# A dense gate matrix built by one-hot matmuls in place of adding scatters, in a Trainium2 encoder layer with product-key experts

## The chip, the cores and the metric

One core of one Trainium2 chip. The metric is device time in microseconds (us) for one execution of the program, taken as the median of several runs.

## The reference, cut to what matters

One encoder layer runs on two sequences, "s" (512 tokens) and "p" (256 tokens), model width 1024. Attention comes first; the part that matters here is the expert layer behind it:

```python
s1 = einsum('thc,hkc->thk', q[:, :, 0], sub_keys_1); s2 = ...    # 8 heads, 128 keys each
v1, i1 = top_k(s1, 16); v2, i2 = top_k(s2, 16)
cand = (v1[..., :, None] + v2[..., None, :]).reshape(T, 8, 256)
top, ci = top_k(cand, 16)
idx = e1 * 128 + e2                     # 8 x 16 = 128 experts of 16384, per token
g = softmax(top)                        # over the 16 of a head
a = gelu(einsum('ted,td->te', expert_u[idx], t))
out = einsum('te,ted->td', g * a, expert_v[idx])
```

For every token 128 of the 16384 experts are chosen, each with a gate g. An expert has a row of u and a row of v, 1024 numbers (4 KB) each.

## The kernel before, in words

**Fronts.** `front("p")` and then `front("s")` do norms, projections, attention, gates, output projection and the query projection of the expert layer. Large products are made of three matmuls (`mm3`, lines 141 to 144): every float32 operand is split by `split` (lines 136 to 139) into a rounded part (ScalarE, line 137) and a rest (VectorE or GpSimd, line 138). At the end of a front `top16` (lines 615 to 621) picks the best 16 of 128 keys for each of 16 half-heads and each tile of 128 tokens.

**Two ways through the experts.** The 256 tokens of p are done by gathers: for each of 2 token tiles, 128 steps fetch one u row for each of 128 tokens (an indirect DMA of 128 x 4 KB, line 782) and reduce it with VectorE (line 789), then 128 steps fetch v rows and accumulate them (line 797). That is 512 gathers. The 512 tokens of s are done densely: stage 1 (`stage1`, lines 714 to 725) computes all 16384 activations in 128 blocks of u, 24 matmuls of 128x512 each, and writes them to `ad` in DRAM; stage 2 (`dense`, lines 727 to 770) reads `ad`, multiplies it with the gate matrix `gd` (line 746) and multiplies by the v blocks, again 128 blocks of 24 matmuls, into eight PSUM tiles `held`.

**The gate matrix.** `gd` holds for every token and expert the gate or zero, 33.5 MB in DRAM, one tensor for each of 4 token tiles. `clear` (lines 700 to 710) fills it with zeros by 16 GpSimd DMAs of 2 MB, woven into the front of p. `pick` (lines 632 to 686), called once for each quarter of the half-heads, makes the indices `si` and gates `wt`; its VectorE steps are the sums `cand` (line 642), `top16`, and for each pair of heads `eq` (line 667), `pr` (line 669) and a reduction (line 670). `scatter` (lines 690 to 698) then issues 512 indirect DMAs from GpSimd's queue, each adding 128 gates of 4 bytes to `gd` (line 696). Stage 2 reads `gd` for 4 blocks at a time (`GRP`), by four DMAs of 256 KB on SyncE's queue (line 737).

**What sets the order.** The program is written as generators that are woven into one another by hand-set rates, and a scheduler then fixes the order of each engine's queue from its own model of times; on the chip each queue is in order. `fill(front("s"), gg, ...)` advances the gathers by 2.25 for every unit of front work. Then 8 blocks of stage 1 are issued (`U0`), the four picks of s carry stage 1 along at 0.45 a unit (`UP`), the 128 steps of four scatters each carry 0.64 blocks of stage 1 (`US`) and 0.44 gathers (`GU`), and the rest of stage 1 follows (lines 848 to 864). `fill(dense(...), gg, GV)` advances 2.2 gathers a v block, and `run(gg)` issues what is left of them. Each gather waits, by a dependence added for pace (line 785), for the last activation that was issued on ScalarE before it. Gathers write into 3 buffers before stage 2 and into 8 in it.

## Time and profile before

| | us |
|---|---|
| median of 3 runs | 2974.01 (2971.81 to 2974.4) |
| the profiled execution, its own time | 2969.84 |
| its span, first to last instruction | 2968.1 |
| mean granted TensorE clock over the span | 0.898 of full speed |

The profiled execution lies 4.2 us under the median, and its time is 1.7 us over its span. PE is the matmul engine TensorE, PEld its weight loads, DVE is VectorE, ACT is ScalarE, POOL is GpSimd, SP is SyncE; a name with a q is the queue of that engine. Matmuls are pipelined and their ends are modelled, so the duration of one is longer than the distance between two.

### The profile page before, as it was taken

Reading aid. Unit: us, or ns where it says so; the run is one execution under the profiler, and the core shown is the slowest. Engines: PE = TensorE matmul, PEld = TensorE weight load, DVE = VectorE, ACT = ScalarE, POOL = GpSimd, SP = SyncE. Lnnn points to the kernel's source line nnn. Section 1 sums busy time; section 2 is a strip of 40 time slices with the busy share of each in tenths; the row PEclk is TensorE's granted clock in tenths of the full one; section 3 lists DMA queues with packets and bytes.
Section 4 is the critical chain, followed back from the end, with each engine's and each line's share of the span. In section 5 each row is a group of like instructions: output and inputs, shape, how many; then the busy total and the mean of one; then the engine's idle time right before and its main releaser. Section 6 shows DMA issues by size and latency. Waiting matters only on the chain.

```text
span 2968.1 us, 31969 instructions
## 1 busy us (share of the span) xinstructions
PE 2334.2 (79%) x10890; PEld 1907.7 (64%) x10890; DVE 1792.2 (60%) x3717; ACT 814.0 (27%) x1315; POOL 1633.8 (55%) x1099
## 2 busy tenths in 40 slices
PE   6899869999987999103666667767999999999950
PEld 5777858778876778102555555555788888888840
DVE  5655896676889992001121212223369989989999
ACT  4554335444322332000111111112222222322210
POOL 0000200555554888888888888886045445544456
PEclk8999989999989999656888888888999999999985
DMA  7875523677862557224565555557679999999999
GB/s 253 284 259 174 161 68 105 206 219 269 283 200 61 121 124 154 18 0 68 115 133 114 127 122 124 116 126 220 222 293 404 402 403 403 394 402 395 397 368 359
DMA packets 311683, 643.06 MB, mean 217 GB/s; under 512 B 98144, under 2 KB 120288, under 8 KB 311520
## 3 DMA queue, kind: packets, MB, share of 16 engines
q0 software_dynamic: 155904, 302.32, 35.4%
q1 hardware_dynamic: 137184, 305.15, 29.7%
...
q14 instruction: 78, 0.64, 0.1%
...
## 4 chain that ended last, share of the span: by engine, by line
PE 32%; POOL 26%; DVE 16%; DMA 14%; issue 10%; ACT 2%; SPq 0%; ACTq 0%; POOLq 0%; DVEq 0%
POOL gd L696 23%; PE held L142 5%; PE held L143 5%; PE held L144 5%; DMA vr<-v 4%; DVE x L797 3%; DMA gr<-u,pidx 2%; DMA wraw<-w_in 2%; POOL gr L782 2%; PE pu L144 2%; DVE gr L789 2%; PE pu L142 2%; PE pu L143 2%; DMA gl<-ad 2%; DMA gd<-wt,si 1%
## 5 line engine op out<-in xcount | busy, mean ns | idle before, releaser
L696 POOL DMA_INDIRECT gd<-wt,si x512 | 881.9, 1722 | 157.1 <-issue 151.8
L144 PE MATMUL pu<-tTh,ul 128*128 128x512 f32 x1024 | 437.6, 428 | 386.5 <-DVE ul L138 386.3
L789 DVE SCALAR_TENSOR_TENSOR gr<-gr,tok 128x1024 f32<-128x1024 f32 x256 | 328.8, 1289 | 489.7 <-DMA gr<-u,pidx 489.1
L782 POOL DMA_INDIRECT gr<-u,pidx x256 | 307.8, 1202 | 419.4 <-ACT ph L137 142.4
L144 PEld LDWEIGHTS pu<-tTh,ul 128*128 128x128 f32 x1024 | 210.0, 205 | 459.2 <-DVE ul L138 414.6
L797 DVE SCALAR_TENSOR_TENSOR x<-gr,act,x 128x1024 f32<-128x1024 f32 x256 | 328.1, 1282 | 289.2 <-DMA gr<-v,pidx 286.1
L782 POOL DMA_INDIRECT gr<-v,pidx x256 | 297.1, 1161 | 321.3 <-ACT ph L137 214.8
L142 PE MATMUL pu<-tTh,uh 128*128 128x512 f32 x1024 | 428.2, 418 | 15.1 <-ACT uh L137 15.1
L143 PE MATMUL pu<-tTl,uh 128*128 128x512 f32 x1024 | 425.0, 415 | 0.0
L143 PE MATMUL held<-vl,ph 128*128 128x512 f32 x1024 | 398.4, 389 | 0.0
L144 PE MATMUL held<-vh,pl 128*128 128x512 f32 x1024 | 398.3, 389 | 0.0
L137 ACT CAST uh<-ur 128x1024 fp32r<-128x1024 f32 x128 | 134.4, 1050 | 905.3 <-PE pu L143 889.0
L142 PE MATMUL held<-vh,ph 128*128 128x512 f32 x1024 | 278.4, 390 | 3.4 <-ACT vh L137 2.7
L138 POOL TENSOR_TENSOR wlo<-wraw,whi 128x1024 fp32r<-128x1024 f32 x51 | 129.8, 2547 | 232.6 <-ACT whi L137 216.4
L142 PEld LDWEIGHTS pu<-tTh,uh 128*128 128x128 f32 x1024 | 210.8, 206 | 60.5 <-ACT uh L137 16.8
L143 PEld LDWEIGHTS pu<-tTl,uh 128*128 128x128 f32 x1024 | 209.8, 205 | 47.8
L142 PEld LDWEIGHTS held<-vh,ph 128*128 128x128 f32 x1024 | 192.0, 188 | 44.7 <-ACT vh L137 3.9
L138 DVE TENSOR_TENSOR ul<-ur,uh 128x1024 fp32r<-128x1024 f32 x128 | 154.0, 1219 | 106.6 <-ACT uh L137 106.6
L144 PEld LDWEIGHTS held<-vh,pl 128*128 128x128 f32 x1024 | 192.3, 188 | 39.9
L143 PEld LDWEIGHTS held<-vl,ph 128*128 128x128 f32 x1024 | 192.2, 188 | 39.9
L137 ACT CAST ph<-gl 128x512 fp32r<-128x512 f32 x128 | 79.6, 622 | 472.3 <-DVE gl L746 402.9
L137 ACT CAST whi<-wraw 128x1024 fp32r<-128x1024 f32 x137 | 143.2, 1048 | 183.6 <-DMA wraw<-w_in 51.5
...
## 6 DMA issues: line engine op xcount, KB each, us to landing
ur<-ublk SPq DMA_DIRECT2D x128, 512.0 KB, 4.0
vr<-v SPq DMA_DIRECT2D x128, 512.0 KB, 11.7
wraw<-w_in SPq DMA_DIRECT2D x80, 512.0 KB, 4.5
...
gt<-gd SPq DMA_DIRECT2D x128, 256.0 KB, 9.1
gl<-ad SPq DMA_DIRECT2D x128, 256.0 KB, 11.2
wraw<-w_query SPq DMA_DIRECT2D x32, 512.0 KB, 4.0
wraw<-w_out SPq DMA_DIRECT2D x16, 512.0 KB, 4.2
```

What stands on the lines that cost most here:

```text
L137: i = ac.copy(hi, src)
L138: eng.tensor_tensor(lo, src, hi.bitcast(F32), op=ALU.subtract)
L142: pe.matmul(out, lhsT=lh, rhs=rh, start=first, stop=False)
L143: pe.matmul(out, lhsT=lh, rhs=rl, start=False, stop=False)
L144: pe.matmul(out, lhsT=ll, rhs=rh, start=False, stop=last)
L696: gp.indirect_dma_start(out=gd[t], out_offset=bass.IndirectOffsetOnAxis(ap=si[:, k:k + 1], axis=0), in_=wt[:, k:k + 1], in_offset=None, co ...
L782: st = gp.indirect_dma_start(out=g, out_offset=None, in_=tab, in_offset=bass.IndirectOffsetOnAxis(ap=pidx[t][:, s:s + 1], axis=0))
L789: ve.scalar_tensor_tensor(g, g, 1.0, tok, op0=ALU.mult, op1=ALU.mult, accum_out=act[:, s:s + 1])
L797: ve.scalar_tensor_tensor(xt, g, act[:, s:s + 1], xt, op0=ALU.mult, op1=ALU.add)
```

## The change

The zero fill and the 512 scatters are gone, and so is `islice`. `pick` now takes one token tile with all 8 heads instead of all token tiles with two heads (the result tiles `vv` and `iu` are laid out to match), two of its steps (`ce` and `pr`) go from VectorE to GpSimd, and it ends with the first index, the second index and the gate of each choice, turned by TensorE so that the choices lie on partitions and the tokens on columns (`sl`). A new function `gbuild` makes, for each token, a 128x128 matrix of first index against second index as one float32 matmul of two one-hot matrices over the 128 choices: `o1` (first index, on VectorE, for 8 tokens at a time) and `o2` (second index times the gate), of which in each 8 tokens 5 are made on VectorE by one instruction and 3 on ScalarE by two. ScalarE copies four tokens out of PSUM together, and each 32 tokens are written to `gd` by one DMA of 2 MB on ScalarE's queue. The order is three picks, a build, a pick, three builds (`ORDER`); a build yields 0.6 for every 4 tokens, which carries 0.6 blocks of stage 1 (`UB`) and 0.9 gathers (`GB`), the latter with 3 more buffers. `gd` is laid out as [16 chunks of 32 tokens, 128, 128, 32], and stage 2 reads it for 8 blocks at a time by one DMA of 2 MB. In stage 2 the gathers have 12 buffers instead of 8, and the pools lie elsewhere in SBUF.

```diff
-GRP = 4
-GR2 = 5
+GCH = 32
+GRP = 8
...
+BY = "avvavvav"
+B1, B2, B3 = 3, 8, 6
...
-U0, UP, US, GU = (8, 0.45, 0.16, 0.11)
-GV = 2.2
+ORDER, SLB = ('pppbpbbb', 3)
+U0, UP, UB = (8, 0.45, 1.0)
+GB, GV = (1.5, 2.2)
...
-    pcol = cp.tile([128, 1], F32, name="pcol")
+    iota = cp.tile([128, 128], F32, name="iota")
...
     sgd = dr.tile([2, 2, 4, 128, 512], F32, name="sgd")
-
-    gd = [dr.tile([128 * 128 * 128, 1], F32, name=f"gd{t}") for t in range(4)]
+    gd = dr.tile([S_S // GCH, 128, 128, GCH], F32, name="gd")
...
-    def pick(pool, seq, c, vv, iu):
...
+    def pick(pool, seq, t, vv, iu):
...
         for i, n in enumerate(CAND[:8]):
-            ve.tensor_tensor(ce[:, :, pos:pos + n], fi[:, :, 1, 0:n], i1[:, :, i:i + 1].broadcast_to([128, n2, n]), op=ALU.add)
+            gp.tensor_tensor(ce[:, :, pos:pos + n], fi[:, :, 1, 0:n], i1[:, :, i:i + 1].broadcast_to([128, 8, n]), op=ALU.add)
             pos += n
-        ve.tensor_tensor(ce[:, :, pos:pos + 8], i1[:, :, 8:16], fi[:, :, 1, 0:1].broadcast_to([128, n2, 8]), op=ALU.add)
...
-        for h in range(n2):
+        for h in range(8):
...
+        for h in range(0, 8, 2):
+            eq = pool.tile([128, 2, NCAND, 16], BF16, tag="eq", name="eq", bufs=2 if seq == "s" else 1)
+            pr = pool.tile([128, 2, 16, NCAND], F32, tag="pr", name="pr", bufs=2 if seq == "s" else 1)
             ve.tensor_tensor(eq, posx.unsqueeze(1).broadcast_to([128, 2, NCAND, 16]),
                              tf[:, h:h + 2, :].unsqueeze(2).broadcast_to([128, 2, NCAND, 16]), op=ALU.is_equal)
-            ve.tensor_tensor(pr, eq.rearrange("p h c s -> p h s c"), ce[:, h:h + 2, :].unsqueeze(2).broadcast_to([128, 2, 16, NCAND]), op=ALU.mult)
+            gp.tensor_tensor(pr, eq.rearrange("p h c s -> p h s c"), ce[:, h:h + 2, :].unsqueeze(2).broadcast_to([128, 2, 16, NCAND]), op=ALU.mult)
             ve.tensor_reduce(ex[:, h:h + 2, :], pr, op=ALU.add, axis=AX.X)
...
-        wt = pool.tile([128, n2, 16], F32, tag=f"wt{c}", name="wt", bufs=1)
-        ve.tensor_tensor(wt, tv, tv[:, :, 0:1].broadcast_to([128, n2, 16]), op=ALU.subtract)
-        gates(pool, wt, n2)
-        si = pool.tile([128, n2 * 16], I32, tag=f"si{c}", name="si", bufs=1)
-        ve.tensor_scalar(si, ex.rearrange("p h s -> p (h s)"), 128.0, pcol, op0=ALU.mult, op1=ALU.add)
-        slots[c] = (si, wt.rearrange("p h s -> p (h s)"))
...
+        ei = pool.tile([128, 128], I32, tag="ei", name="ei", bufs=1)
+        ve.tensor_copy(ei, ex.rearrange("p h s -> p (h s)"))
+        ii = pool.tile([128, 128], I32, tag="ii", name="ii", bufs=1)
+        for z in range(2):
+            if z == 0:
+                ve.tensor_single_scalar(ii, ei, 7, op=ALU.logical_shift_right)
+            else:
+                ve.tensor_single_scalar(ii, ei, 127, op=ALU.bitwise_and)
+            ve.tensor_copy(e[z].rearrange("p h s -> p (h s)"), ii)
+        p = ps_tr("p_sl")
+        for j, src in enumerate((e[0], e[1], wt)):
+            pe.transpose(p[:, j * 128:(j + 1) * 128], src.rearrange("p h s -> p (h s)"), ident)
+        sl[t] = [slp[0].tile([128, 128], F32, tag=f"sl{j}", name=f"sl{j}", bufs=SLB) for j in range(5)]
+        for j in range(3):
+            ac.copy(sl[t][j], p[:, j * 128:(j + 1) * 128])
+        for j in range(1, 3):
+            ac.mul(sl[t][2 + j], p[:, j * 128:(j + 1) * 128], -1.0)
         yield 2
 
...
-    def scatter(c):
-
-        si, wt = slots[c]
-        for s in range(32):
-            for t in range(4):
-                k = t * 32 + s
-                gp.indirect_dma_start(out=gd[t], out_offset=bass.IndirectOffsetOnAxis(ap=si[:, k:k + 1], axis=0),
-                                      in_=wt[:, k:k + 1], in_offset=None, compute_op=ALU.add)
-            yield 1
...
-    def clear():
-
-        z = gpl.tile([128, D], F32, tag="gr", name="zero", bufs=3)
-        gp.memset(z, 0.0)
-        for t in range(4):
-            v = gd[t].rearrange("(p q k d) o -> q p k (d o)", p=128, q=4, d=D)
-            for q in range(4):
-                st = gp.dma_start(v[q], z.unsqueeze(1).broadcast_to([128, 4, D]))
-                if anchor[0] is not None:
-                    tc.add_manual_dep(st.ins, anchor[0].ins.name, SYNC, reason="pace")
-                yield 0
+    def gbuild(pool, t):
+        for c in range(128 // GCH):
+            gs = pool.tile([128, 128, GCH], F32, tag="gs", name="gs", bufs=2)
+            for q in range(0, GCH, 4):
+                p = (ps_tr, ps_o)[q // 4 % 2]("p_g")
+                t4 = c * GCH + q
+                if q % 8 == 0:
+                    o1 = pool.tile([128, 8, 128], F32, tag="o1", name="o1", bufs=B1)
+                    ve.tensor_tensor(o1, iota.unsqueeze(1).broadcast_to([128, 8, 128]),
+                                     sl[t][0][:, t4:t4 + 8].unsqueeze(2).broadcast_to([128, 8, 128]), op=ALU.is_equal)
+                for j in range(4):
+                    tk = t4 + j
+                    tg = {"a": "o2a", "v": "o2"}[BY[tk % len(BY)]]
+                    o2 = pool.tile([128, 128], F32, tag=tg, name=tg, bufs=B2 if tg == "o2" else B3)
+                    if tg == "o2a":
+                        ac.activation(o2, iota, AF.Abs, bias=sl[t][3][:, tk:tk + 1])
+                        ac.activation(o2, o2, AF.Relu, bias=sl[t][2][:, tk:tk + 1], scale=sl[t][4][:, tk:tk + 1])
+                    else:
+                        ve.tensor_scalar(o2, iota, sl[t][1][:, tk:tk + 1], sl[t][2][:, tk:tk + 1], op0=ALU.is_equal, op1=ALU.mult)
+                    pe.matmul(p[:, j * 128:(j + 1) * 128], lhsT=o1[:, q % 8 + j, :], rhs=o2, start=True, stop=True)
+                ac.copy(gs[:, :, q:q + 4].rearrange("p e t -> p t e"), p.rearrange("p (t e) -> p t e", e=128))
+                yield 0.6
+            nc.scalar.dma_start(gd[t * (128 // GCH) + c], gs)
...
-                for t in range(4):
-                    nc.sync.dma_start(gts[g][:, t], gd[t].rearrange("(p e t) o -> p e (t o)", e=128, t=128)[:, g * GRP:(g + 1) * GRP, :])
+                gts[g] = pv_.tile([128, S_S // GCH, GRP, GCH], F32, tag="gt", name="gt", bufs=2)
+                nc.sync.dma_start(gts[g], gd[:, :, g * GRP:(g + 1) * GRP, :].rearrange("c p e t -> p c e t"))
...
-            gv = ga.rearrange("p (t k) -> p t k", k=128)
+            gv = ga.rearrange("p (c t) -> p c t", t=GCH)
...
-            more = len(gp2) and s % (GR2 + 3) >= 3
-            g = (gp2[0] if more else pool).tile([128, D], F32, tag="gr2" if more else "gr", name="gr", bufs=GR2 if more else 3)
+            more, n = gp2[-1]
+            own = s % (n + 3) < 3
+            g = (pool if own else more).tile([128, D], F32, tag="gr" if own else "gr2", name="gr", bufs=3 if own else n)
...
     gpl = ctx.enter_context(tc.tile_pool(name="ga", bufs=1, side="right", reuse_waits="tile"))
-    zero = clear()
-    fill(front("p"), zero, 0.5)
-    run(zero)
+    run(front("p"))
     def picks_p():
-        for c in range(4):
-            yield from pick(pks["p"][1], "p", c, *tops["p"][c])
+        for t in range(2):
+            yield from pick(pks["p"][1], "p", t, *tops["p"][t])
         pks["p"][0].__exit__(None, None, None)
...
-    due, gdue = [0.0], [0.0]
-    for c in range(4):
-        fill(pick(pks["s"][1], "s", c, *tops["s"][c]), ua, UP, due)
-    for c in range(4):
-        for _ in scatter(c):
-            due[0] += US * 4
-            gdue[0] += GU * 4
-            while due[0] >= 1.0:
-                due[0] -= 1.0
-                next(ua, None)
-            while gdue[0] >= 1.0:
-                gdue[0] -= 1.0
-                next(gg, None)
-    run(ua)
+    with tc.tile_pool(name="gb", bufs=1, reuse_waits="tile") as gpool:
+        slp.append(gpool)
+        gp2.append((gpool, 3))
+        P = [pick(pks["s"][1], "s", t, *tops["s"][t]) for t in range(4)]
+        B = [gbuild(gpool, t) for t in range(4)]
+        due = [0.0]
+        it = {"p": iter(P), "b": iter(B)}
+        for k in ORDER:
+            g = next(it[k])
+            fill(weave(g, gg, GB) if k == "b" else g, ua, UP if k == "p" else UB, due)
+        run(ua)
+        gp2.append((None, 0))
     pks["s"][0].__exit__(None, None, None)
     psx[0].__exit__(None, None, None)
-    gp2.append(ctx.enter_context(tc.tile_pool(name="gr2", bufs=1, side="right", reuse_waits="tile")))
+    ux.__exit__(None, None, None)
+    gp2.append((ctx.enter_context(tc.tile_pool(name="gr2", bufs=1, reuse_waits="tile")), 9))
     psd = ctx.enter_context(tc.tile_pool(name="psd", bufs=1, space=PSUM))
-    pv_ = ctx.enter_context(tc.tile_pool(name="dv", bufs=1, reuse_waits="tile"))
+    pv_ = ctx.enter_context(tc.tile_pool(name="dv", bufs=1, side="right", reuse_waits="tile"))
     fill(dense(pv_, psd), gg, GV)
     run(gg)
```

## Rows read from the trace of the kernel before

**Rows 1.** Windows: length, busy time (x instructions) of PE, PEld, DVE, ACT, POOL, clock, DMA share, GB/s.

```profile
966.00:1196.00 230.00, 218.42 (x943) 176.53 (x943) 162.35 (x452) 72.10 (x94) 199.81 (x100) 0.99 0.60 133
1196.00:1369.00 173.00, 1.69 (x8) 1.07 (x6) 0.00 (x0) 1.54 (x2) 144.65 (x94) 0.52 0.23 2
1369.00:2047.00 678.00, 467.73 (x1706) 364.30 (x1706) 145.87 (x148) 109.77 (x143) 568.55 (x360) 0.85 0.58 123
2047.00:2160.00 113.00, 103.91 (x432) 83.37 (x431) 41.42 (x39) 30.49 (x40) 14.40 (x11) 0.96 0.68 244
2160.00:2862.00 702.00, 697.18 (x3072) 576.13 (x3070) 627.75 (x779) 199.47 (x251) 346.00 (x279) 1.00 1.01 390
2862.00:2968.00 106.00, 0.00 (x0) 0.00 (x0) 99.66 (x79) 0.00 (x0) 70.96 (x69) 0.52 0.94 369
```

**Rows 2.** Waits from 1380 to 2047 us: engine line, whom for, total us, times, longest.

```profile
DVE x L797 <- DMA gr<-v,pidx: 274.5, 26, 15.9
DVE gr L789 <- DMA gr<-u,pidx: 252.5, 23, 15.8
...
PE pu L144 <- DVE ul L138: 195.3, 48, 8.0
```

**Rows 3.** Groups by form: busy us, mean ns of one, idle before and its releasers.

```profile
L696 POOL DMA_INDIRECT gd<-wt,si x512 | 881.9, 1722 | 157.1 <-issue 151.8 <-DMA gd<-wt,si 4.0 <-DVE vv L620 1.3
...
L137 ACT CAST uh<-ur 128x1024 fp32r<-128x1024 f32 x128 | 134.4, 1050 | 905.3 <-PE pu L143 889.0 <-PE pu L144 6.6 <-DVE ti L618 4.4
...
L138 POOL TENSOR_TENSOR wlo<-wraw,whi 128x1024 fp32r<-128x1024 f32 x51 | 129.8, 2547 | 232.6 <-ACT whi L137 216.4 <-DVE iu L621 5.3 <-DVE vv L617 5.3
L138 DVE TENSOR_TENSOR wlo<-wraw,whi 128x1024 fp32r<-128x1024 f32 x86 | 109.5, 1276 | 88.4 <-ACT whi L137 87.9
...
L669 DVE TENSOR_TENSOR pr<-eq,ce 128x1600 f32<-128x1600 bf16 x24 | 79.3, 3303 | 0.0
...
L439 ACT ACTIVATE sm<-sm,nm 128x256 f32<-128x256 f32 x56 | 28.4, 507 | 37.7 <-DVE nm L488 20.5 <-DVE nm L515 11.2 <-DVE es L525 3.3
...
L609 ACT COPY ss<-p_s 128x512 f32<-128x512 f32 x16 | 9.4, 587 | 58.4 <-DVE s L619 47.5 <-PE p_s L607 10.9
```

**Rows 4.** Timeline of PE around four float32 matmuls of 128x128 (start, us, instruction).

```profile
948.13 1.05 PE L607 MATMUL p_s<-kys,qT 128*128 128x128 f32 x8
948.94 0.48 PE L144 MATMUL pq<-tTh,wlo 128*128 128x512 f32 x1
949.25 0.40 PE L142 MATMUL pq<-tTh,whi 128*128 128x512 f32 x1
```

**Rows 5.** Instructions on single tiles: duration ns min/median/max, first and last start.

```profile
L138 DVE TENSOR_TENSOR ul<-ur,uh x128: 1192/1220/1285, 967.6 to 2149.0; 128x1024 fp32r<-128x1024 f32 x128
...
L684 DVE TENSOR_SCALAR si<-ex,pcol x4: 256/268/344, 945.4 to 1110.2; 128x128 int32<-128x128 f32 x4
...
L642 DVE TENSOR_TENSOR cand<-vv x64: 142/173/2405, 318.1 to 1049.8; 128x16 f32<-128x16 f32 x16, 128x8 f32<-128x8 f32 x12, 128x32 f32<-128x32 f32 x8, 128x64 f32<-128x64 f32 x8
```

**Rows 6.** Gathers issued: up to 945, 1370 to 2047 (two), from 2860 (durations ns, starts).

```profile
L782 POOL DMA_INDIRECT gr<-u,pidx x104: 932/940/1987, 500.9 to 859.8; - x104
...
L782 POOL DMA_INDIRECT gr<-v,pidx x26: 997/1000/1003, 1698.2 to 2039.5; - x26
L782 POOL DMA_INDIRECT gr<-u,pidx x23: 1000/1001/1009, 1387.6 to 1688.2; - x23
...
L782 POOL DMA_INDIRECT gr<-v,pidx x70: 936/1016/1861, 2859.5 to 2954.9; - x70
```

**Rows 7.** DMA issues (count, KB, median us to landing): 0 to 220 us, 220 to 500, 500 to 950.

```profile
wraw<-w_in SPq DMA_DIRECT2D x39, 512.0 KB, 6.5
...
wraw<-w_in SPq DMA_DIRECT2D x26, 512.0 KB, 3.7
...
gr<-u,pidx POOLq DMA_INDIRECT x104, 5.6
```

**Rows 8.** Waits of the first 220 us: engine line, whom for, total us, times, longest.

```profile
ACT whi L137 <- DMA wraw<-w_in: 41.3, 16, 4.7
```

More of the change, by code (lines that the diff above doesn't have):

```diff
@@ L1 @@
 from contextlib import ExitStack
-from itertools import islice
 import numpy as np
@@ L581, in front @@
             pp = fs.enter_context(tc.tile_pool(name="wq" + seq, bufs=1, side="right" if seq == "p" else "left", reuse_waits="tile"))
-            vv = [pk.tile([128, nt, 4, 16], F32, tag=f"vv{c}", name="vv") for c in range(4)]
-            iu = [pk.tile([128, nt, 4, 16], U32, tag=f"iu{c}", name="iu") for c in range(4)]
+            vv = [pk.tile([128, 16, 16], F32, tag=f"vv{t}", name="vv") for t in range(nt)]
+            iu = [pk.tile([128, 16, 16], U32, tag=f"iu{t}", name="iu") for t in range(nt)]
             for c in range(4):
@@ L610, in front @@
                     for t in range(nt):
-                        top16(pp, ss[:, t, :], 128, vv[c][:, t, m, :], iu[c][:, t, m, :])
+                        top16(pp, ss[:, t, :], 128, vv[t][:, hh, :], iu[t][:, hh, :])
                     yield 0
@@ L621, in top16, with gates @@
         ve.max_index(out=i[:, 8:16], in_max=v[:, 8:16], in_values=s2[:, :n])
-    def gates(pool, w, n=8):
+    def gates(pool, w):
         ac.activation(w, w, AF.Exp)
-        sm = pool.tile([128, n], F32, tag="gsm", name="gsm", bufs=1)
+        sm = pool.tile([128, 8], F32, tag="gsm", name="gsm", bufs=1)
         ve.tensor_reduce(sm, w, op=ALU.add, axis=AX.X)
         ve.reciprocal(sm, sm)
-        ve.tensor_tensor(w, w, sm.unsqueeze(2).broadcast_to([128, n, 16]), op=ALU.mult)
-    def pick(pool, seq, c, vv, iu):
-        nt = 4 if seq == "s" else 2
-        n2 = 2 * nt
-        fi = pool.tile([128, n2, 2, 16], F32, tag="fi", name="fi", bufs=1)
-        ac.copy(fi.rearrange("p h z k -> p (h z) k"), iu.rearrange("p t m k -> p (t m) k"))
-        v4 = vv.rearrange("p t (h z) k -> p (t h) z k", z=2)
-        cand = pool.tile([128, n2, NCAND], F32, tag="cand", name="cand", bufs=1)
+        ve.tensor_tensor(w, w, sm.unsqueeze(2).broadcast_to([128, 8, 16]), op=ALU.mult)
@@ L640, in pick @@
+    def pick(pool, seq, t, vv, iu):
+        fi = pool.tile([128, 8, 2, 16], F32, tag="fi", name="fi", bufs=1)
+        ac.copy(fi.rearrange("p h z k -> p (h z) k"), iu)
+        v4 = vv.rearrange("p (h z) k -> p h z k", z=2)
+        cand = pool.tile([128, 8, NCAND], F32, tag="cand", name="cand", bufs=1)
         pos = 0
         for i, n in enumerate(CAND[:8]):
-            ve.tensor_tensor(cand[:, :, pos:pos + n], v4[:, :, 1, 0:n], v4[:, :, 0, i:i + 1].broadcast_to([128, n2, n]), op=ALU.add)
+            ve.tensor_tensor(cand[:, :, pos:pos + n], v4[:, :, 1, 0:n], v4[:, :, 0, i:i + 1].broadcast_to([128, 8, n]), op=ALU.add)
@@ L650, in pick @@
+        tv = pool.tile([128, 8, 16], F32, tag="tv", name="tv", bufs=1)
+        ti = pool.tile([128, 8, 16], U32, tag="ti", name="ti", bufs=1)
+        ce = pool.tile([128, 8, NCAND], F32, tag="ce", name="ce", bufs=1)
+        i1 = pool.tile([128, 8, 16], F32, tag="i1", name="i1", bufs=1)
         ac.mul(i1, fi[:, :, 0, :], 128.0)
@@ L672, in pick @@
         if seq == "p":
-            for t in range(nt):
-                k = slice(32 * c, 32 * c + 32)
-                h = slice(2 * t, 2 * t + 2)
-                ve.tensor_tensor(pw[t][:, k].rearrange("p (h s) -> p h s", s=16), tv[:, h, :], tv[:, h, 0:1].broadcast_to([128, 2, 16]), op=ALU.subtract)
-                ve.tensor_copy(pidx[t][:, k], ex[:, h, :].rearrange("p h s -> p (h s)"))
+            ve.tensor_tensor(pw[t].rearrange("p (h s) -> p h s", s=16), tv, tv[:, :, 0:1].broadcast_to([128, 8, 16]), op=ALU.subtract)
@@ new lines, in pick @@
+        ve.tensor_tensor(wt, tv, tv[:, :, 0:1].broadcast_to([128, 8, 16]), op=ALU.subtract)
+        gates(pool, wt)
+        ei = pool.tile([128, 128], I32, tag="ei", name="ei", bufs=1)
+        ve.tensor_copy(ei, ex.rearrange("p h s -> p (h s)"))
+        ii = pool.tile([128, 128], I32, tag="ii", name="ii", bufs=1)
+        for z in range(2):
+            if z == 0:
[3 more added lines that the diff above has]
+            ve.tensor_copy(e[z].rearrange("p h s -> p (h s)"), ii)
@@ L923, in _layout @@
     o["posx"] = np.broadcast_to(np.arange(NCAND).astype(ml_dtypes.bfloat16)[:, None], (128, NCAND, 16))
-    o["pcol"] = np.arange(128, dtype=np.float32)[:, None]
+    o["iota"] = np.broadcast_to(np.arange(128, dtype=np.float32), (128, 128))
     o["maskA_s"], o["maskB_s"], o["maskO_s"] = _masks(_SEQ_S, _PERM_S[:128], 4)
```

33 lines of the change are left out of this document (17 added, 16 removed).

## The prediction

> **What bounds the kernel now.** I read the windows by stage first, then the waits of the longest stage, then the costs of single groups. The windows [rows 1] show that the stretch between the fronts and stage 2, from 966 to 2160 us, takes 1194 us for work that TensorE does elsewhere in little over half of that: stage 2 has the same 3072 matmuls of 128x512 and does them in 702 us, 0.229 us each, at clock 1.00 (2.4 GHz). In the stretch there are three different states. Up to 1196 stage 1 runs beside the picks at 943 matmuls in 230 us, 0.244 us each. From 1196 to 1369 TensorE, VectorE and ScalarE all stand still, and the granted clock of idle TensorE is 0.52, close to the lower of its two levels (1.2 GHz). From 1369 to 2047 TensorE has 1706 matmuls in 678 us, 0.397 us each, at 0.85, while GpSimd is busy for 569 of them.
>
> Who holds whom is in the waits [rows 2]: VectorE waits 274.5 and 252.5 us for gathered rows, and TensorE waits for `ul`, a VectorE product that stands behind those waits in VectorE's queue. The gathers are late because they stand in GpSimd's queue among the scatters, 512 of 1.72 us with 157.1 us of idle time before them, 2.03 us each [rows 3]. So the scatters pace the stretch through the gathers, and TensorE is not the bound. Once the last scatter is out at 2047, the remaining matmuls go at 432 in 113 us, 0.262 us each [rows 1]. Stage 2 is bound by TensorE and by transfers nearly equally (DMA share 1.01), and behind it stands a tail of 106 us in which only gathers run [rows 1].
>
> **The change, part by part.** *The stretch.* The scatters go, 1039 us of GpSimd time. What is late next is TensorE. Its work is 128 blocks of 24 matmuls and 512 new float32 matmuls of 128x128, in 128 groups of four. The trace has four matmuls of this form in one piece (eight records) [rows 4]: from their start to the start of the second matmul behind them are 1.12 us, of which one 128x512 matmul takes 0.23, so a group of four costs 0.89. The bounds are 0.81 (to the start of the first matmul behind) and 1.05 (the piece's own length). At the full rate the work is 702 + 128 x 0.89 = 816 us. I take the rate at which stage 1 ran beside the picks, 0.244 instead of 0.229, because there too VectorE and ScalarE had much other work: 3072 x 0.244 + 114 x 0.244/0.229 = 871 us, and 3 for twelve transposes, 874. Gain: 1194 - 874 = **320 us**.
>
> This holds if no other engine needs more. VectorE: `ul` 128 x 1.22 = 156 us; `o1` is a two-input operation of the same shape, 64 x 1.22 = 78; `o2` is nearest to the 128x128 operation with a scalar, 320 x 0.268 = 86 [rows 5]; gathers, 112 at no more than 106/70 = 1.5 us (the tail over its gathers), 168 [rows 1, 6]; picks and `top16` no more than the 162 us of the first window less the `ul` of its 39 blocks, 115 [rows 1]. That is 603 of 874. ScalarE: 128 casts of 1.05 and as many activations of 128x512, about 0.59 like the copy, 210 us; 192 tokens with two instructions, each at most the 0.507 of the 128x256 activation with its own bias, 195; 128 copies of 0.587, 75 [rows 3]; 480 of 874. The copies write with a stride of 128 bytes, which no row shows: as fast as the copy, or, bounded by the slowest row of that group, 1.05 us each, 60 us more, which still hides. GpSimd: the gathers and 16 products `pr`. A product costs 3.30 us on VectorE, and the same subtraction is 2547 ns on GpSimd against 1276 on VectorE [rows 3], so 6.6 us, 106 us together, hidden behind stage 1 as long as VectorE, which waits for each, has other work queued. Transfers: u 67 MB, `ad` 34, the new `gd` writes 34, gathers 112 x 0.52 = 58; 193 MB in 874 us is 221 GB/s, against 390 in stage 2 [rows 1]. On SyncE's queue 128 reads of `gd` become 16; on ScalarE's queue 16 writes of 2 MB are added, each behind the copy that fills it, so ScalarE waits for nothing there.
>
> *Gathers.* The fronts issued 104 [rows 6]. The picks of p now make 22 steps instead of 24, so two more fit, 106. The scatters carried 128 x 0.44 = 56, the builds carry 28 each, 112. Stage 2 carries 281 in both. So 106 + 112 + 281 = 499 of 512 are out by its end and 13 are left where 70 were. They came out at 95.4 us for 70, 1.36 us each [rows 6], so the tail of 106 us loses 57 x 1.36 = **77 us** and 29 remain.
>
> *Stage 2.* The matmuls are the same. The reads of `gd` come as 2 MB every 8 blocks in pieces of 1 KB, before as four times 256 KB every 4 blocks in pieces of 2 KB; with more gather buffers the transfers may start earlier. TensorE is hardly ever short of data now. I take **5 us more**. The bounds: no change below, and above, if these 33.5 MB took twice as long as at 390 GB/s, 86 us more, since transfers already fill the stage [rows 1].
> The page DMA: Bandwidth & Descriptors of the Trainium skill (Latency and other measured facts) says that copies whose row pitch is a large power of two lose bandwidth, 164 GB/s at 2 MiB against 207 at 512 KiB. In the new layout 16 pieces lie 2 MiB apart for each partition, so by that rule the 86 us would become about 108, an estimate of 22 us more from that page's figures; no run here shows such a pitch yet.
>
> *Front of p.* Its transfers lose 33.5 MB of zeros. The weight tiles landed in 6.5 us there and in 3.7 behind it [rows 7], and ScalarE waited 41.3 us for them [rows 8]. I take 15 us of gain, 41.3 x (1 - 3.7/6.5) = 18 less a little, as some of these waits are hidden; bounds 0 and 41. `pr` of the p picks, 8 products, goes to GpSimd with one buffer: 8 x 3.3 us less on VectorE against 8 x 6.6 that it waits; -26 to +26 us, taken as nothing, since fronts have other work for VectorE.
>
> *Sum.* 2968 - 15 - 320 + 5 - 77 = 2561 us of span; the profiled execution would be 1.7 above it, 2563, and the median of the runs shown lies 4 above the profiled execution: **2567 us**.
>
> **The rivals.** *Build stalls.* Every group of four needs three engines in turn, and all queues are in order. If TensorE were fed only 80% of the time, the stretch would be 816/0.8 = 1020 us, 146 more: 2713. For it: at 0.262 us a matmul the end of the stretch ran at 87% even without scatters. Against it: 0.244 beside saturated picks, and stage 2 at full rate with VectorE busy 628 of 702 us [rows 1].
>
> *The picks wait for GpSimd.* VectorE then pays 6.6 instead of 3.3 us for each of 16 products, and 53 us come on top where the picks are longer than the blocks of stage 1 they carry: about 2620. For it: a sum `cand` of 0.173 us at the median took up to 2.405 [rows 5], about the length of one GpSimd subtraction, so the two engines do hold each other up. Against it: two buffers, and 31 blocks of stage 1 to do meanwhile.
> The page SBUF — State Buffer of the Trainium skill (SBUF: two separate sides) calls the port pair of GpSimd and VectorE an exclusive lock; by that the waits would be whole instructions, as that 2.405 suggests.
>
> *Stage 2 becomes bound by transfers.* The `gd` reads take twice their time: 86 us instead of 5, about 2648. For it: the share is 1.01 already. Against it: the same bytes, and before, too, they came in bursts.
>
> *Slower: gathers hold VectorE again.* 112 gathers are woven into the builds, and each stands in VectorE's queue. From 1369 to 2047 49 gathers took 678 us, 13.8 us each [rows 6]; at that price 112 need 1550 us and the kernel takes about 3240. It decides from the point where a gather's turn takes longer than (874 + 401)/112 = 11.4 us. Against it: that price was six scatters between two gathers. In the fronts a gather landed in 5.6 us [rows 7]; with 1.0 for its issue [rows 6] they need, even one at a time, 112 x 6.6 = 739 us, under the 874, and there are six buffers.
>
> *It doesn't do what it says.* If not the scatters but stage 1 itself paced the stretch, the tail's 77 us and the front's 15 would be won and 5 lost, and the build's 117 us would lie partly in TensorE's gaps: 2887 to 3004, with no change in between. The rate after the last scatter and the standstill speak against it.
>
> **How the numbers follow.** Forecast 0.60 (2567), build stalls 0.12 (2713), picks 0.12 (2620), transfers 0.10 (2648), slower 0.05, no effect 0.01. All but the last two are faster: 0.94; 0.2% is 6 us, about what a measurement can tell from no change; same 0.01, slower 0.05. The range: below, full rate with groups of 0.81 (806 us, -68) and the front's larger gain (-20), 2479; above, the build stalls, 2713. I give 2480 to 2715.
>
> **What would show it.** Right: no idle stretch of TensorE between fronts and stage 2, which starts near 1825 us; clock 0.97 or more there; about 13 gathers behind stage 2, in some 30 us; stage 2 near 705 us; groups of four at 0.8 to 1.05 us; VectorE busy 60 to 75% in the builds. Wrong: waits of VectorE for gathered rows that repeat the old table; `pr` on GpSimd far over 6.6 us with VectorE idle behind it; stage 2 over 730 us with TensorE waiting on `gl`; ScalarE's strided copies well over 1 us.

## The result and the profile after

The changed kernel takes 2575.52 us (median of 4 runs, 2570.95 to 2582.16) against 2972.91 us before in the same comparison: ratio 0.867, 95% interval 0.864 to 0.869. The forecast was 2567. The profiled execution took 2570.95 us, its span is 2569.1, the mean granted clock 0.963. The sum came out 8 us from the forecast one, but two of its terms missed by over 50 us each.

The windows of the kernel after, cut where its stages change (columns as in [rows 1], which has the same stages of before):

```profile
0.00:220.00 220.00, 199.74 (x1131) 162.52 (x1132) 143.22 (x388) 131.19 (x244) 0.70 (x6) 0.98 0.45 140
...
897.00:1100.00 203.00, 162.24 (x660) 129.60 (x659) 196.44 (x528) 71.81 (x121) 91.41 (x52) 0.90 0.29 99
1100.00:1700.00 600.00, 598.37 (x3132) 512.43 (x3132) 384.85 (x582) 369.65 (x664) 150.20 (x112) 1.00 0.76 268
1700.00:1781.00 81.00, 75.72 (x322) 61.51 (x320) 27.44 (x27) 24.53 (x32) 0.94 (x1) 0.96 0.76 281
1781.00:2540.00 759.00, 719.16 (x3072) 588.58 (x3072) 630.18 (x782) 197.11 (x251) 346.45 (x287) 0.97 0.99 364
2540.00:2569.00 29.00, 0.00 (x0) 0.00 (x0) 24.36 (x21) 0.00 (x0) 7.67 (x7) 0.53 0.59 232
```

Stage 1 begins at 897 instead of 966. The picks of s (to 1100) fill VectorE, 196 of 203 us. In the builds (1100 to 1700) TensorE is full at clock 1.00, which is 2.4 GHz; nothing is left of the standstill. Stage 2 is longer than before, 759 instead of 702 us, at 364 instead of 390 GB/s. The tail shrank from 106 to 29 us.

| stage | forecast, us | measured, us | difference |
|---|---|---|---|
| fronts, to the first matmul of stage 1 | 951 | 897 | -54 |
| stretch | 874 | 884 | +10 |
| stage 2 | 707 | 759 | +52 |
| tail | 29 | 29 | 0 |
| span | 2561 | 2569 | +8 |

How a group of four float32 matmuls stands in the builds, in TensorE's timeline of the kernel after (start, us, instruction):

```profile
1500.74 0.38 PE L723 MATMUL p_g<-o2a,o 128*128 128x128 f32 x2
1500.96 0.61 PE L723 MATMUL p_g<-o,o 128*128 128x128 f32 x4
1501.41 0.39 PE L723 MATMUL p_g<-o2a,o 128*128 128x128 f32 x2
1501.55 0.48 PE L144 MATMUL pu<-tTh,uh 128*128 128x512 f32 x1
1501.87 0.40 PE L145 MATMUL pu<-tTl,uh 128*128 128x512 f32 x1
```

Measured as the forecast measured it, from the start of the group to the start of the second matmul behind it (1.13 us) less the 0.23 of one matmul of stage 1, a group costs 0.90 us; the forecast had 0.89. To the start of the first matmul behind it are 0.81, the forecast's lower bound.

Stage 2's waits in the kernel after (engine line, whom for, total us, times, longest):

```profile
DVE gl L761 <- DMA gl<-ad: 104.2, 14, 9.8
...
PE held L144 <- ACT vh L139: 37.0, 14, 6.0
```

VectorE waits for `ad` 14 times; stage 2 has 16 reads of `gd`, one for each 8 blocks. So these came first among the suspects. By the windows, TensorE stands idle 40 us of the stage (759 less 719) instead of 5 (702 less 697), and the same 3072 matmuls keep it busy 22 us longer, because its clock falls in the waits (0.97 over the stage instead of 1.00; 0.50, the level of 1.2 GHz, from 1928 to 1932 us, where one of the waits lies). Two rows of stage 2 show eight equal matmuls in a stretch without a wait, and behind a wait of 6 us:

```profile
1919.54 1.98 PE L144 MATMUL held<-vh,ph 128*128 128x512 f32 x8
1931.10 3.59 PE L144 MATMUL held<-vh,ph 128*128 128x512 f32 x8 [5.96 <-ACT vh L139]
```

### The profile page after: what moved, and what is told of

Read it like the earlier page. It is cut to its first block, busy times and chain, and to the rows that moved or that the text cites. A ratio compares the mean times of both kernels' runs of the same rounds, so it can differ in the third digit from the quotient of the medians.

```text
span 2569.1 us, 34289 instructions
## 1 busy us (share of the span) xinstructions
PE 2380.3 (93%) x11926; PEld 1983.1 (77%) x11926; DVE 1934.7 (75%) x3989; ACT 1064.2 (41%) x1848; POOL 895.3 (35%) x648
## 4 chain that ended last, share of the span: by engine, by line
PE 43%; issue 20%; DVE 16%; DMA 10%; POOL 9%; ACT 2%; SPq 0%; POOLq 0%; ACTq 0%; DVEq 0%
POOL gr L799 8%; PE pu L146 7%; PE pu L145 6%; PE pu L144 6%; PE p_g L723 4%; DMA gl<-ad 4%; DMA gr<-u,pidx 2%; DMA wraw<-w_in 2%; PE held L144 2%; DVE wlo L140 2%; PE held L145 2%; PE pq L145 2%; PE pq L146 2%; PE held L146 1%; PE pq L144 1%
## 5 line engine op out<-in xcount | busy, mean ns | idle before, releaser
L799 POOL DMA_INDIRECT gr<-v,pidx x256 | 315.8, 1233 | 660.0 <-ACT ph L139 175.6
L146 PE MATMUL pu<-tTh,ul 128*128 128x512 f32 x1024 | 409.8, 400 | 37.9 <-DVE ul L140 37.9
L144 PE MATMUL pu<-tTh,uh 128*128 128x512 f32 x1024 | 411.6, 402 | 3.7 <-ACT uh L139 3.7
L145 PE MATMUL pu<-tTl,uh 128*128 128x512 f32 x1024 | 405.4, 396 | 0.0
L144 PE MATMUL held<-vh,ph 128*128 128x512 f32 x1024 | 290.1, 408 | 37.7 <-ACT vh L139 37.0
L146 PEld LDWEIGHTS pu<-tTh,ul 128*128 128x128 f32 x1024 | 196.7, 192 | 83.6 <-DVE ul L140 43.1
L144 PEld LDWEIGHTS pu<-tTh,uh 128*128 128x128 f32 x1024 | 197.0, 192 | 42.5 <-ACT uh L139 4.6
L145 PEld LDWEIGHTS pu<-tTl,uh 128*128 128x128 f32 x1024 | 196.5, 192 | 39.4
L140 DVE TENSOR_TENSOR ul<-ur,uh 128x1024 fp32r<-128x1024 f32 x128 | 171.5, 1340 | 56.9 <-ACT uh L139 53.8
L761 DVE TENSOR_TENSOR gl<-gl,gt 128x512 f32<-128x512 f32 x128 | 88.2, 689 | 111.0 <-DMA gl<-ad 110.9
## 6 DMA issues: line engine op xcount, KB each, us to landing
gt<-gd SPq DMA_DIRECT2D x16, 2048.0 KB, 21.4
```

The costliest lines, as they stand in the source:

```text
L140: eng.tensor_tensor(lo, src, hi.bitcast(F32), op=ALU.subtract)
L144: pe.matmul(out, lhsT=lh, rhs=rh, start=first, stop=False)
L145: pe.matmul(out, lhsT=lh, rhs=rl, start=False, stop=False)
L146: pe.matmul(out, lhsT=ll, rhs=rh, start=False, stop=last)
L761: ve.tensor_tensor(gv, gv, gts[g][:, :, b, :], op=ALU.mult)
L799: st = gp.indirect_dma_start(out=g, out_offset=None, in_=tab, in_offset=bass.IndirectOffsetOnAxis(ap=pidx[t][:, s:s + 1], axis=0))
```

## The experiments

Every ratio is against the kernel before on the same chip. Differences in us are against the 2575.52 of the changed kernel, which was timed on another occasion; the medians of before lie between 2969 and 2973 us on these occasions, so some 4 us of such a difference may come from that.

**Do the scatters pace the stretch?** In the kernel before, `scatter` issues nothing:

```diff
-                k = t * 32 + s
-                gp.indirect_dma_start(out=gd[t], ..., in_=wt[:, k:k + 1], ..., compute_op=ALU.add)
+                pass
```

> The kernel before with the 512 scatters left out: the gate matrix stays at its zeros, everything else is issued in the same weave, so the dense part of the output lacks its gates. Theory (the scatters in GpSimd's queue pace the gathers, the gathers hold VectorE, VectorE holds TensorE): the stretch between the fronts and stage 2 falls from 1194 us to 750-820 us, with no standstill, and the total to 2540-2620 us, the tail of about 100 us staying. Rival (each gather's own turn holds VectorE, whatever else GpSimd does): 56 gathers at over 10 us keep the stretch above 1000 us and the total above 2770 us.

One time of 2493.66 us. Windows of stretch, stage 2 and tail:

```profile
963.00:1683.00 720.00, 705.44 (x3083) 577.66 (x3082) 351.54 (x638) 214.17 (x279) 71.66 (x60) 1.00 0.59 196
1683.00:2386.00 703.00, 697.39 (x3072) 576.41 (x3072) 628.19 (x780) 199.48 (x252) 348.38 (x279) 1.00 1.01 390
2386.00:2492.00 106.00, 0.00 (x0) 0.00 (x0) 99.03 (x78) 0.00 (x0) 71.35 (x69) 0.51 0.94 364
```

The stretch drops from 1194 to 720 us, below the 750 expected: stage 1 beside picks and gathers runs at almost the rate of stage 2. Stage 2 and tail stay. So the scatters cost 474 us of the stretch, and with the builds in their place it stands 164 over that floor (884 - 720), of which the forecast's 114 for the new matmuls are the larger part. This is one execution.

**The front.** The zero fill is put back, into tensors that nobody reads:

```diff
-    run(front("p"))
+    zero = clear()
+    fill(front("p"), zero, 0.5)
+    run(zero)
```

> The changed kernel with the old fill of 33.5 MB of zeros put back into the front of p, into a spare tensor that nobody reads. Stage 1 began at 897 us instead of 966, 69 us earlier, where 15 were forecast. Theory A (about half of it is the zero fill, which slowed the weight tiles of the front of p): the prompt's normed tiles leave the front 25-35 us later and the total is 2600-2615 us. Theory B (the zero fill cost hardly anything, the gain is the new grouping of the picks): at most 10 us later, total 2570-2588 us. Forecast's own size: 15 us, 2590 us.

2610.71 us, ratio 0.880 (0.877 to 0.884): 35 us more than the changed kernel, as theory A has it. Its first 220 us, the whole front, and the stretch:

```profile
0.00:220.00 220.00, 185.35 (x957) 148.51 (x958) 124.45 (x365) 111.51 (x219) 13.77 (x23) 0.90 0.77 269
...
0.00:933.00 933.00, 840.86 (x4745) 701.75 (x4746) 673.23 (x2051) 397.00 (x777) 313.63 (x207) 0.95 0.61 203
933.00:1820.00 887.00, 840.64 (x4112) 705.74 (x4110) 608.63 (x1137) 465.87 (x817) 241.97 (x165) 0.97 0.65 230
```

The fill is worth 36 of the 69 us by which stage 1 starts earlier (933 against 897; in the ten other runs of the changed kernel it starts between 893 and 905). In the first 220 us TensorE gets 1131 instructions done without it and 957 with it. The other 33 us are no gain of the front. The rows of `wt`, whose subtraction stands near the end of a pick, and of `p_s`, the query scores of the front (durations in ns, first and last start), of before:

```profile
L681 DVE TENSOR_TENSOR wt<-tv x4: 258/272/274, 899.6 to 1079.8; 128x128 f32<-128x128 f32 x4
...
L607 PE MATMUL p_s<-kys,qT x192: 270/275/583, 307.6 to 979.5; 128*128 128x128 f32 x192
```

and after:

```profile
L683 DVE TENSOR_TENSOR wt<-tv x4: 270/284/3793, 927.6 to 1078.9; 128x128 f32<-128x128 f32 x4
...
L609 PE MATMUL p_s<-kys,qT x192: 270/275/377, 274.9 to 896.9; 128*128 128x128 f32 x192
```

Before, the first pick, of two heads, was at its end (899.6) while the front still had scores to make (to 979.5). A pick of all 8 heads begins behind the last score (896.9), so all the picks now lie in the stretch. That is read from the two traces; no run undid the regrouping. The other change in the front, `pr` of the p picks on GpSimd, is not the reason: with `pr` back on VectorE (the next run) stage 1 starts at 896.

**Do the picks wait for GpSimd?** `pr` and `ce` go back to VectorE:

```diff
-            gp.tensor_tensor(ce[...], ...)
+            ve.tensor_tensor(ce[...], ...)
...
-            gp.tensor_tensor(pr, ...)
+            ve.tensor_tensor(pr, ...)
```

> The changed kernel with the products pr and the sums ce of the picks back on VectorE (24 products of 3.3 us there instead of 4.9 us on GpSimd). Theory A (a GpSimd operation that reads SBUF holds up VectorE's two-input operations for its whole length, so the move relieved nothing): total between 2555 and 2580 us, the long VectorE operations of 4-5 us beside pr gone, and the first 200 us of the stretch no slower. Theory B (the move takes 16 x 3.3 = 53 us off a saturated VectorE): the first part of the stretch grows by 25-50 us, total 2600-2625 us.

2551.97 us, ratio 0.860 (0.857 to 0.862): 24 us faster, a little beyond theory A's range (the two ratios differ by 0.007, some 20 us). VectorE has more work and is done sooner. Its timeline in the kernel after, and GpSimd's at the same time:

```profile
931.78 0.31 DVE L619 MAX8 tv<-cand 128x8 f32<-128x50 f32 x2
932.01 4.24 DVE L140 TENSOR_TENSOR ul<-ur,uh 128x1024 fp32r<-128x1024 f32 x1
936.18 0.31 DVE L619 MAX8 tv<-cand 128x8 f32<-128x50 f32 x2
...
936.76 3.93 DVE L632 TENSOR_TENSOR wt<-wt,gsm 128x128 f32<-128x128 f32 x1
...
930.09 10.45 POOL L674 TENSOR_TENSOR pr<-eq,ce 128x1600 f32<-128x1600 bf16 x2 [8.55 <-DVE eq L672]
```

A `ul` of 1.22 us lasts 4.24, and a product of 128x128 that takes 0.29 lasts 3.93, each beside a `pr` on GpSimd; both have two tensors as inputs. The `max` between them, with one, keeps its time (0.31 for two, before the first and behind it). The page SBUF — State Buffer of the Trainium skill (SBUF: two separate sides) calls the port pair of the two engines an exclusive lock: of a GpSimd instruction that reads SBUF and a VectorE instruction with two SBUF inputs, the one that starts first holds it to its end and the other waits. The trace agrees: the first `pr` ends at 935.18 and `ul` 1.07 us later, the second at 940.55 and the product 0.14 later. The second `pr`, which starts at 935.13, lasts 5.42 us where the shortest lasts 4.35, longer by about what `ul` runs on into it. Groups of the picks' part (columns as in [rows 3]), 897 to 1100 us of the kernel after:

```profile
L674 POOL TENSOR_TENSOR pr<-eq,ce 128x1600 f32<-128x1600 bf16 x16 | 79.9, 5007 | 73.7 <-DVE eq L672 66.6 <-DVE tv L622 7.1
L140 DVE TENSOR_TENSOR ul<-ur,uh 128x1024 fp32r<-128x1024 f32 x27 | 48.3, 1788 | 4.7 <-ACT uh L139 4.7
L722 DVE TENSOR_SCALAR o<-iota,sl,sl 128x128 f32<-128x128 f32 x20 | 27.5, 1392 | 0.7 <-PE p_g L723 0.7
```

and 896 to 1074 us of this run, with its window:

```profile
L674 DVE TENSOR_TENSOR pr<-eq,ce 128x1600 f32<-128x1600 bf16 x15 | 48.1, 3233 | 0.0
L140 DVE TENSOR_TENSOR ul<-ur,uh 128x1024 fp32r<-128x1024 f32 x25 | 30.4, 1217 | 0.0
...
L722 DVE TENSOR_SCALAR o<-iota,sl,sl 128x128 f32<-128x128 f32 x18 | 5.5, 338 | 0.0
...
896.00:1074.00 178.00, 155.74 (x663) 123.97 (x662) 177.86 (x566) 71.83 (x121) 0.00 (x0) 0.94 0.33 111
```

About the same matmuls (663 against 660) take 178 instead of 203 us. Some `o2`, with one tensor and two columns of scalars, were held as well: 1392 ns at the mean against 338, with a median of 341 and a longest of 4724.

**Stage 2: what slows it?** First the layout: `gd` is turned so that a read finds one row of 16 KB for each partition.

```diff
-    gd = dr.tile([S_S // GCH, 128, 128, GCH], ...)
+    gd = dr.tile([128, 128 // GRP, S_S // GCH, GRP, GCH], ...)
-            nc.scalar.dma_start(gd[t * (128 // GCH) + c], gs)
+            nc.scalar.dma_start(gd[:, :, t * (128 // GCH) + c], gs.rearrange("p (g b) t -> p g b t", b=GRP))
-                nc.sync.dma_start(gts[g], gd[:, :, g * GRP:(g + 1) * GRP, :].rearrange("c p e t -> p c e t"))
+                nc.sync.dma_start(gts[g], gd[:, g])
```

> The changed kernel with the gate matrix laid out so that stage 2 reads 16 KB in one piece per partition (the 1 KB pieces move to the write in the builds). Stage 2 took 759 us in the changed kernel instead of 702. Theory A (the 1 KB pieces 2 MiB apart make the reads slow in a stage that transfers already fill): stage 2 falls to 700-720 us, its rate returns to 390-400 GB/s, the total falls by 40-60 us to 2515-2535 us. Theory B (it is the size of the burst, 2 MB in one DMA ahead of the blocks' own loads on SyncE's queue): stage 2 stays above 740 us and the total within 10 us of 2575. In both, the builds may grow by up to 10 us for the writes in pieces.

2510.99 us, ratio 0.846 (0.844 to 0.849): 65 us faster. Its stage 2:

```profile
1775.00:2475.00 700.00, 696.61 (x3072) 576.50 (x3072) 634.77 (x783) 197.74 (x252) 348.55 (x287) 1.00 1.01 395
```

The read of 2 MB stays, so its size alone is not the cause; with the layout turned the whole loss goes. The stretch, where the writes now come in pieces, takes 879 us, so they cost nothing there. Nor are short pieces alone the cause: the kernel before read pieces of 2 KB, 1 MB at a time in four transfers that landed in 9.1 us at the median, and its stage 2 took 702 us. What costs is the pieces of 1 KB, as they lie, in a read of 2 MB. SyncE's queue shows a trace of it. In the kernel after, the issue behind a read of `gd` takes 11 us:

```profile
1904.11 0.37 SPq L752 DMA_DIRECT2D gt<-gd  x1
1905.89 11.14 SPq L756 DMA_DIRECT2D gl<-ad  x1
```

and with whole rows 0.32:

```profile
1889.06 0.32 SPq L752 DMA_DIRECT2D gt<-gd  x1
1891.26 0.32 SPq L756 DMA_DIRECT2D gl<-ad  x1
```

Four runs then asked which side of the layout it is. The pitch:

```diff
-    gd = dr.tile([S_S // GCH, 128, 128, GCH], ...)
+    gdp = dr.tile([S_S // GCH, 128 * 128 * GCH + 1024], ...)
+    gd = gdp[:, 0:128 * 128 * GCH].rearrange("c (p e t) -> c p e t", p=128, e=128)
```

> The changed kernel with 4 KB of unused space behind each of the 16 chunks of gd, so that the 16 pieces of one partition lie 2 MB + 4 KB apart instead of 2 MB; pieces of 1 KB and everything else stay. Theory A, stage 2 lost its 52 us to the pitch of a power of two: stage 2 falls to 700 to 720 us, total 2515 to 2535. Theory B, it lost them to the shortness of the pieces: stage 2 stays at 750 to 765 us, total within 10 us of 2575.

2614.63 us, ratio 0.880 (0.879 to 0.882): 39 us slower, which neither theory had. Stage 2 takes 779 us from its first to its last matmul, the stretch 896. So breaking the pitch won nothing, and no run speaks for the pitch as the cause; as the padding costs time of its own, for a reason that was not found, the run doesn't rule the pitch out either. The rule that the prediction weighed, of the page DMA: Bandwidth & Descriptors of the Trainium skill (Latency and other measured facts), was measured on another pitch, that from one partition's row to the next. In this layout that pitch is 16 KB, and the 2 MB lie between the 16 pieces of one partition. Padding of 4 KB, which that page of the Trainium skill gives as the remedy, did not help here: 779 us against 756.

The length of a piece, 2 KB instead of 1 (the 8 pieces of a partition then lie 4 MB apart, so the run changes the pitch as well):

```diff
+    gd = dr.tile([S_S // GCH // 2, 128, 128 // GRP, 2, GRP, GCH], ...)
+            nc.scalar.dma_start(gd[(t * (128 // GCH) + c) // 2, :, :, c % 2], gs.rearrange("p (g b) t -> p g b t", b=GRP))
+                nc.sync.dma_start(gts[g], gd[:, :, g].rearrange("c p k e t -> p c (k e t)"))
```

> gd laid out so that stage 2 finds 2 KB in one piece, 8 pieces for each partition of a 2 MB read (changed kernel: 16 pieces of 1 KB; the run that reads whole rows: one row of 16 KB). Theory A, the number of pieces counts: the issue behind a read of gd, 8 to 12 us on SyncE's queue in the changed kernel and 0.3 in the run with whole rows, shrinks with the 16384 pieces that are left of 32768, and stage 2 falls most of the way, to 700 to 725 us, total 2510 to 2540. Theory B, anything short of one row per partition pays: stage 2 stays over 740 us, total over 2555.

2565.31 us, ratio 0.863 (0.861 to 0.866), 10 us faster at the most, and the two intervals overlap: theory B. The queue's stall is nearly gone, as the next issues show, and stage 2 still takes 745 us from its first to its last matmul:

```profile
1907.73 0.37 SPq L752 DMA_DIRECT2D gt<-gd  x1
1909.51 1.27 SPq L756 DMA_DIRECT2D gl<-ad  x1
1910.87 2.01 SPq L754 DMA_DIRECT2D vr<-v  x1
```

So the 11 us of the issue were a sign and not the cause. In the next run `gd` is read on ScalarE's queue:

```diff
-                nc.sync.dma_start(gts[g], ...)
+                nc.scalar.dma_start(gts[g], ...)
```

> The changed kernel with the 16 reads of gd issued on ScalarE's queue instead of SyncE's; same pieces, same layout. Theory A, the cost of the pieces is that SyncE's queue takes in no further issue for some 10 us behind each read of gd, so that ad and v for the next blocks come late: on another queue they are issued in time, the waits of VectorE for ad (104 us) go, and stage 2 falls to 700 to 720 us, total 2515 to 2535. Theory B, the pieces are slow in the transfer engines themselves, whatever queue they come from: stage 2 stays at 745 to 765 us, total within 12 us of 2575.

2584.88 us, ratio 0.871 (0.868 to 0.873): the number of theory B, within 12 us. The wait only changes its name. ScalarE waits for v rows as often and as long as VectorE waited for `ad`, and SyncE's queue waits for the read of `gd`:

```profile
ACT vh L139 <- DMA vr<-v: 99.8, 15, 10.7
...
SPq L754 <- DMA gt<-gd: 213.7, 13, 20.0
```

So the run did not make the condition that theory A names: 13 times SyncE's queue stood for up to 20 us until a read of `gd` had landed, although that read was on another queue, and v came late as before. Why it waits there is not shown, and the run doesn't decide between the theories.

The landing times say which reads are slow: after 21.4 us in the kernel after, in pieces of 2 KB 20.8, on ScalarE's queue 34.4, in whole rows (the last run below) 11.3 us, at the median. `ad` and v have three buffers each and a block of stage 2 takes 5.4 us (697/128), so some 16 us are covered, an estimate. Around the read issued at 1904 the queues of the kernel after move this:

```profile
1904.00:1928.00 24.00, 21.14 (x94) 17.17 (x92) 14.86 (x23) 4.72 (x6) 8.27 (x7) 0.99 1.04 393
1928.00:1944.00 16.00, 12.90 (x50) 10.54 (x51) 15.38 (x22) 4.72 (x6) 7.34 (x6) 0.80 0.94 343
```

and with whole rows, around the read issued at 1889:

```profile
1889.00:1913.00 24.00, 24.00 (x108) 19.87 (x107) 22.00 (x34) 7.75 (x10) 12.18 (x10) 1.00 1.03 411
1913.00:1929.00 16.00, 16.00 (x72) 13.27 (x71) 15.13 (x24) 4.40 (x7) 7.02 (x7) 1.00 1.03 406
```

Over the last 13 reads of each run, the 24 us from the issue move 387 GB/s at the mean with pieces of 1 KB and 409 with whole rows, the 16 us behind them 331 and 405. So the read itself runs at a rate some 5% lower, and over two thirds of the bytes that are missing are missing behind it, where TensorE is short of data and its clock falls. That speaks for lateness as the larger part, with a lower throughput beside it; no run separates the two. It led to the last run on this, which was to split and spread the read:

```diff
-                nc.sync.dma_start(gts[g], gd[:, :, g * GRP:(g + 1) * GRP, :]...)
+                    nc.sync.dma_start(gts[n][:, 4 * k:4 * k + 4], gd[4 * k:4 * k + 4, :, n * GRP:(n + 1) * GRP, :]...)
```

> The changed kernel with the same layout and pieces of 1 KB, but the 2 MB for the next 8 blocks are read in four transfers of 512 KB, one in each of the blocks 3 to 6 of the 8 before, instead of one of 2 MB. Theory A, the burst: while a read of 2 MB is under way (21 us) the queue moves nearly its full 390 GB/s, but ad and v, with three buffers each, come late, and the time is lost because the transfers fall idle behind it; in smaller parts nothing comes late, and stage 2 falls to 700 to 720 us, total 2515 to 2540. Theory B, the throughput: pieces of 1 KB cost the transfer engines more than whole rows wherever they stand, and stage 2 stays at 745 to 765 us, total 2560 to 2590.

2583.36 us, ratio 0.872 (0.869 to 0.875), stage 2 at 766 us by the same measure. This run did not try what it was meant to. The scheduler put the four parts next to one another in SyncE's queue:

```profile
2006.15 6.38 SPq L754 DMA_DIRECT2D gt<-gd  x4
2012.62 2.53 SPq L758 DMA_DIRECT2D gl<-ad  x1
```

It shows that four transfers in a row are no better than one. Whether short pieces spread over the blocks would cost anything stays open.

**Are the gathers in the builds hidden?**

```diff
-GB, GV = (1.5, 2.2)
+GB, GV = (0.0, 2.2)
```

> The changed kernel with no gathers woven into the builds; all of them are left for stage 2 and the tail. Theory A, gathers in the builds are hidden under TensorE, which is full there: the stretch keeps its 875 to 884 us, and 112 more gathers at 1.36 us stand in the tail, 152 us, about 2725 us. Theory B, the gathers hold VectorE or the transfers in the builds: the stretch falls by 20 us or more, below 865 us, and the total is 2660 to 2705.

One time of 2723.05 us, against 2725. Its stretch, stage 2 and tail:

```profile
898.00:1784.00 886.00, 838.33 (x4114) 704.41 (x4113) 480.30 (x1007) 466.62 (x817) 94.88 (x55) 0.97 0.47 164
1784.00:2541.00 757.00, 720.55 (x3072) 589.83 (x3070) 624.56 (x793) 197.18 (x251) 345.89 (x284) 0.97 0.99 363
2541.00:2721.00 180.00, 0.08 (x1) 0.00 (x0) 171.17 (x140) 0.31 (x1) 123.15 (x120) 0.51 0.95 370
```

112 gathers in the builds cost nothing there (886 against 884 us) and 151 us in the tail (180 against 29), 1.35 us each. This is one execution.

**Versions that beat both kernels.** The diffs of the whole rows and of the products on VectorE together:

> Both edits that were faster alone, together: stage 2 reads the gate matrix in whole rows, and pr and ce of the picks are made on VectorE. Theory A, the two gains lie in different stages (stage 2, 65 us; the picks and the builds, 24 us) and add up: 2575 - 65 - 24 = about 2487 us, stretch 855 to 865, stage 2 at 697 to 707. Theory B, one of them uses up what the other wins (a transfer that both bring forward): over 2500 us.

2488.25 us, ratio 0.837 (0.836 to 0.838): the two gains add up (stretch 862, stage 2 697 us). Besides both diffs:

```diff
-ORDER, SLB = ('pppbpbbb', 3)
+ORDER, SLB = ('pbpbpbpb', 3)
```

> As the run with both edits, and each pick is followed at once by its build, four times, instead of three picks first. Theory A, the first 180 us of the stretch are bound by VectorE (busy 178 of 178 us) while in the builds TensorE is full and VectorE has a third of its time free, but a pick still stands alone in VectorE's queue for its length: the time moves little, within 15 us of the run with both. Theory B, the scheduler mixes a pick with the build before it, and VectorE's work of the picks is hidden under TensorE's of the builds: the stretch shortens by 20 to 40 us, about 2450 to 2465 us.

2485.84 us, ratio 0.837 (0.835 to 0.838): no difference that can be told. Instead of that, besides both diffs:

```diff
-GB, GV = (1.5, 2.2)
+GB, GV = (1.9, 2.2)
```

> The run with both edits, with 1.9 instead of 1.5 gathers for each unit of the builds, 146 instead of 115 of them there. Theory A, gathers in the builds stay hidden under TensorE and the tail loses all its gathers: 8 last sums, the last transfer and no more, some 10 us instead of 32, total 2488 - 22 = about 2466 us. Theory B, more gathers hold up the builds or their buffers: the stretch grows by as much as the tail loses, 2480 to 2490 us.

2465.96 us, ratio 0.831 (0.830 to 0.832), the best found. Its stretch, stage 2 and what is behind:

```profile
897.00:1762.00 865.00, 833.83 (x4113) 699.97 (x4112) 642.70 (x1224) 465.79 (x818) 208.66 (x146) 0.98 0.73 256
1762.00:2461.00 699.00, 696.61 (x3072) 576.50 (x3072) 612.52 (x769) 201.61 (x252) 325.28 (x260) 1.00 0.97 380
2461.00:2463.50 2.50, 0.00 (x0) 0.00 (x0) 0.00 (x0) 0.00 (x0) 0.00 (x0) 0.85 0.22 81
```

146 gathers stand in the builds, where the run before had 112 (its plan says 115), 260 in stage 2, and no tail is left.

## Why the prediction was right in its total and wrong in two terms

- *What bounds.* Right. Scatters paced the stretch: without them it takes 720 us. TensorE came next, as forecast: 598 of 600 us in the builds. The rivals in which the builds stall, or nothing changes, fell.
- *Stretch, 874.* Measured 884, by another route. The rate of 0.244 was spread evenly in the forecast. In fact the builds run at the full rate with groups at 0.90 where 0.89 was forecast, and the loss sits in the picks: the 609 matmuls of stage 1 there at 0.229 us are 139, five groups 5, and the part takes 203. The forecast took the picks' VectorE time from the window that begins at 966, so without the part that ran ahead of it; by the traces they now all lie in the stretch. That a term built on an even rate came out within 10 us is in part luck.
- *`pr` on GpSimd.* The duration was 4.86 us at the median, not 6.6, and lay outside TensorE's path as such. What failed is "hidden behind stage 1 as long as VectorE has other work queued": much of that work is held as well. The rival of the picks was right that the two engines hold each other up; the move costs 24 us, against the 53 that it priced.
- *VectorE and ScalarE in the builds.* `o2` took 0.34 us where 0.268 was taken, the strided copies 1.12 us at the median (1058 to 1204 ns), just over the upper bound of 1.05 rather than the 0.587 taken. Both were hidden, as said: VectorE is busy 64% and ScalarE 62% of the builds.
- *Gathers, 77 us of gain.* Right: 29 us are left, and the run without gathers in the builds gives 1.35 us each. The longer stage 2 carried 287 gathers instead of the 281 counted, so 7 are left instead of 13, and 21 sums on VectorE fill the rest of the tail.
- *Stage 2, +5.* The term that failed. It is +57, inside its bounds of 0 and 86; the value near the lower end rested on "TensorE is hardly ever short of data now". The rival "stage 2 becomes bound by transfers" was the nearest to what happened, at two thirds of its price, and "stage 2 over 730 us" is one of the prediction's own signs of being wrong. Shown is that the layout in pieces of 1 KB costs it when 2 MB are read at once: with whole rows the stage takes 700 us. That it does so because the read lands in 21 instead of 11 us and what stands beside it comes late is argued from rates and landing times; length, pitch and burst were not separated.
- *Front, -15.* Mis-sized. The fill alone is worth 36, inside the bounds of 0 and 41. The forecast priced ScalarE's waits for weights; TensorE's clock in the first 220 us is also higher, 0.98 against 0.90 with the fill put back, which those waits don't show. The other 33 us of the earlier start are, as the traces are read above, work that moved into the stretch. In the lower end of the range the front's larger gain is taken as 20 us, where the bound of 41 gives 26; that moves the end by 6 us.
- The differences of front and stage 2, -54 and +52, cancel. That the total is within 9 us of 2567 is to that extent luck.
